# One score product for both heads of a feature tile, and value products on alternating column halves

## Chip, cores and metric

The kernel runs on one core of one Trainium2 chip. The metric is the time of one execution on the device, in microseconds (us); three runs of the kernel before give a median of 3754.48 us (3749.0 to 3759.8). The core has five engines with a queue each: TensorE (PE, matrix products, with weight loads shown apart as PEld), VectorE (DVE), ScalarE (ACT), GpSimd (POOL) and SyncE (SP, which here issues DMA transfers).

## What is computed

The reference is two transformer blocks on 256 tokens of width 2048, all in fp32. The parts that matter here are the two attentions. The first block's attention has an indexer of 8 heads that picks at most 64 keys for each query, and 16 heads of 64 features over keys and values that are expanded from a shared latent:

```python
score = einsum('bqhs,bqh->bqs', relu(einsum('bqhd,bsd->bqhs', qi, ik)), wi)
...
logits = einsum('bqhr,bqkr->bqhk', ql, c_sel) * SA_SCALE + bias
pr = softmax(where(valid, logits, -inf))
o_lat = einsum('bqhk,bqkr->bqhr', pr, c_sel)
```

The second block's attention has 32 query heads of 64 features, four key and value heads (8 query heads share one), a window of 128 keys and a sink per head. Around them stand large projections, a recurrent part (RWKV) and a mixture of experts in the first block, and a state space layer (Mamba) in the second.

## The kernel before, in words

Features lie on the 128 partitions, tokens along the free dimension. A feature tile of 128 partitions holds two heads of 64 features: head 2p in partitions 0 to 63 and head 2p+1 in partitions 64 to 127.

The projections run in `gemm` (line 170): weights come by DMA in `wload`, `wsplit` splits them into a high part on ACT (line 139) and a low part on DVE (line 141), and PE multiplies with the activations (lines 204 and 206, PSUM tile `g`); `gemm_rows` does the same with tokens as rows (lines 227 to 229). Attention works in fp32 without a split, and the profile shows each such product as two passes over the moving columns.

An attention **unit** is one pair of heads and one half of the queries (`tt` 0 or 1, 128 queries each). With `tt` = 0 it has 128 keys, with `tt` = 1 it has 256. A unit of `Dsa.run` (first block) goes like this:

- line 812 loads the bias of both heads (tile `bm`) by a DMA that ACT issues, and line 814 adds the mask on POOL;
- line 819 makes the scores into PSUM tile `psL`, one product for each head, with the 64 partitions of that head as contraction;
- lines 821 to 829 (DVE and ACT) add, take the maximum, exponentiate and normalise;
- line 834 transposes the probabilities on PE into `psP`, and line 836 copies them out on ACT (`pT`);
- line 842 makes the values' products into `psO`, with 64 output partitions for each head;
- lines 846 and 847 write the result as a high and a low part to `o2b` on ACT and DVE.

The pair of a unit are two heads of the same parity, from two neighbouring feature tiles (line 809), so both products of a unit use the same 64 partitions: of the keys as contraction at line 819, and of `psO` as output at line 842. Each head has its own columns in PSUM. `Swa.attend` (second block) does the same for 32 heads: scores at line 1825 (`psl`), softmax at 1831 to 1840, transposes at 1845 (`psp`), values at 1852 (`pso`), and one DVE copy at 1854 into `o`. The indexer of the first block multiplies at line 773 (`psI`) in the same way. There are 16 units in the first block, 32 in the second, and 8 pairs of indexer products.

Keys are prepared once: `ikd` (lines 755 to 757) and `kT` (788 to 796, from `psK`, written by ACT) in the first block, `kd` (1731, filled by DMA at line 1798) in the second. Values `vr` follow `kT` (797 to 805, from `psV`).

`weave` keeps up to three units going and takes one stage of each in turn. All of attention's products share two PSUM banks (tag `m`). The order in each engine's queue is laid out when the kernel is compiled: a scheduler puts instructions that are ready earlier in front of those that are traced before them, so products of the next projections stand between those of the units. Each engine takes its queue in order.

Line 1528 is part of the Mamba layer and isn't touched by the diff; its products have 64 output columns, and consecutive ones (`e` in 0, 1) write different halves of the PSUM partitions:

```python
for ch in range(2):
    for e in range(2):
        E.matmul(ps[64 * e:64 * e + 64, ch * 128:(ch + 1) * 128], lhsT=xd[:, ch, hA + e, :],
                 rhs=M[ch][:, 2 * u + e, :], start=True, stop=True)
```

Of the kernel before, what the change touches and what calls it, by code (L numbers as in the profile page):

```python
# [9 lines left out]
F32 = mybir.dt.float32  # L10
# [4 lines left out]
AF = mybir.ActivationFunctionType  # L15
ALU = mybir.AluOpType
# [4 lines left out]
T = 256  # L21
# [11 lines left out]
DECAY_C = math.exp(-0.5)  # L33
QUAD = "(a b i)"
# [657 lines left out]
SA_SCALE = 64 ** -0.5  # L692
# [18 lines left out]
class Dsa:  # L711
# [23 lines left out]
    def run(self):  # L735
        k, nc, pool, par, c = self.k, self.k.nc, self.pool, self.par, self.k.c
        V, S, P, E = nc.vector, nc.scalar, nc.gpsimd, nc.tensor
# [17 lines left out]
        ikd = pool.tile([128, T], F32, name="ikd")  # L755
        V.tensor_copy(ikd[64:128], kwT[64:128])
        nc.scalar.dma_start(ikd[0:64], kwT[64:128])
# [6 lines left out]
        for tt in range(2):  # L764
            nk = 128 * (tt + 1)
            sc = pool.tile([128, T], F32, name=f"sc{tt}")
            P.memset(sc, 0.0)
            for hq in range(4):
                ps = k.bank("psI")
                for j in range(2):  # L770
                    h = 4 * (hq // 2) + 2 * j + hq % 2
                    hs = slice(64 * (h % 2), 64 * (h % 2) + 64)
                    E.matmul(ps[:, j * 256:j * 256 + nk], lhsT=iqT[h // 2][hs, tt * 128:(tt + 1) * 128],
                             rhs=ikd[hs, 0:nk], start=True, stop=True)
                for j in range(2):
                    h = 4 * (hq // 2) + 2 * j + hq % 2
                    rl = W("rl", [128, T])[:, :nk]
                    V.tensor_scalar(rl, ps[:, j * 256:j * 256 + nk], 0.0, iw[:, tt, h:h + 1], op0=ALU.max, op1=ALU.mult)
# [28 lines left out]
        def unit(tt, hq):  # L807
            nk = 128 * (tt + 1)
            hs_ = [4 * (hq // 2) + 2 * j + hq % 2 for j in range(2)]
            bm = W("bm", [128, 2, T], 3)[:, :, :nk]  # L810
            src = self.bd
            nc.scalar.dma_start(bm, bass.AP(tensor=src.tensor, offset=src.offset + hs_[0] * 512 + 128,
                                            ap=[[1, 128], [1024, 2], [1, nk]]))
            P.tensor_tensor(bm, bm, neg[tt][:, None, :].to_broadcast([128, 2, nk]), op=ALU.add)
            ps = k.bank("psL")
            pv = ps.rearrange("p (j s) -> p j s", j=2)[:, :, :nk]
            for j, h in enumerate(hs_):
                hs = slice(64 * (h % 2), 64 * (h % 2) + 64)
                E.matmul(pv[:, j], lhsT=qT[h // 2][hs, tt * 128:(tt + 1) * 128], rhs=kT[hs, h // 2, T - nk:],
                         start=True, stop=True)  # L820
# [23 lines left out]
            j0, pv = hs_[0] // 2, ps[hs, 0:256].rearrange("p (j t) -> p j t", j=2)  # L844
            hi = self.o2[hs, j0:j0 + 2, tt * 128:(tt + 1) * 128]
            S.copy(hi, pv)
            V.tensor_tensor(self.o2[hs, j0:j0 + 2, T + tt * 128:T + (tt + 1) * 128], pv, hi.bitcast(F32), op=ALU.subtract)

        weave((unit(tt, hq) for tt in range(2) for hq in range(8)), 3, 1)


# [872 lines left out]
class Swa:  # L1724
    def __init__(self, k, par, pool, q):
        self.k, self.par, self.pool, self.q = k, par, pool, q
        nc, a = k.nc, k.a
        self.c = k.load_consts(pool, "const_swa", _SWA)
        self.rot = pool.tile([128, 128], F32R, name="rotr")
        self.o = pool.tile([128, 16, T], F32, name="o")  # L1730
        self.kd = pool.tile([128, 4, T], F32, name="kd")
        self.vr = pool.tile([128, 2, 256], F32, name="vr")
        sk = a["b_sinks_2"]
        self.sk = pool.tile([128, 32], F32, name="sk")
        nc.scalar.dma_start(self.sk, bass.AP(tensor=sk.tensor, offset=sk.offset, ap=[[0, 128], [1, 32]]))

    def tables(self):
# [7 lines left out]
        ang = pool.tile([128, T], F32, name="ang")  # L1745
# [3 lines left out]
        n = pool.tile([128, T], F32, name="nper")  # L1749
# [37 lines left out]
    def evict_kv(self, col, ps):  # L1787
# [25 lines left out]
    def attend(self):  # L1813
# [3 lines left out]
        def unit(hq, tt):  # L1817
            hs_ = [4 * (hq // 2) + 2 * j + hq % 2 for j in range(2)]
            hs = slice(64 * (hq % 2), 64 * (hq % 2) + 64)
            kv = hs_[0] // 8  # L1820
            nk = 128 * (tt + 1)
            ps = k.bank("psl")
            pv = ps.rearrange("p (j s) -> p j s", j=2)[:, :, :nk]
            for j, h in enumerate(hs_):
                E.matmul(pv[:, j], lhsT=self.q[hs, h // 2, tt * 128:(tt + 1) * 128], rhs=self.kd[hs, kv, 0:nk],  # L1825
                         start=True, stop=True)
# [4 lines left out]
            P.tensor_copy(bt[:, :, nk], self.sk[:, hs_[0]:hs_[0] + 3:2])  # L1831
# [17 lines left out]
            ps = k.bank("pso")  # L1849
            for j, h in enumerate(hs_):  # L1850
                for s in range(tt + 1):
                    E.matmul(ps[hs, j * 128:(j + 1) * 128], lhsT=self.vr[:, s, kv * 64:kv * 64 + 64], rhs=pT[:, j, s],  # L1852
                             start=(s == 0), stop=(s == tt))
            V.tensor_copy(self.o[hs, hs_[0] // 2:hs_[0] // 2 + 2, tt * 128:(tt + 1) * 128],
                          ps[hs, 0:256].rearrange("p (j t) -> p j t", j=2))

        weave((unit(hq, tt) for hq in range(16) for tt in range(2)), 3, 1)
# [209 lines left out]
```

## Time and profile before

| | |
|---|---|
| median of three runs | 3754.48 us (3749.0 to 3759.8) |
| the profiled execution | 3757.85 us |
| its span, first to last instruction | 3756.1 us |
| instructions | 56311 |
| PE busy | 3634.1 us, 97% of the span |
| weight loads busy | 3023.4 us, 80% |
| DVE, ACT, POOL busy | 2671.5, 1985.7, 1320.7 us |
| granted TensorE clock, mean | 0.992 |

A row of the time order gives the start, the time from the first start to the last end, the engine, the line, the operation, the tiles written and read, the form and the count. The form `64*128 64x256` is a product with 64 contraction partitions and 128 output partitions over 256 moving columns; `128*64` has 64 output partitions. A row with "x4" merges four such instructions that follow each other. Matmuls are pipelined, so that starts of neighbours lie closer than one's length.

### The profile page before, as it was taken

Reading aid. Unit: us, or ns where it says so; the run is one execution under the profiler, and the core shown is the slowest. Engines: PE = TensorE matmul, PEld = TensorE weight load, DVE = VectorE, ACT = ScalarE, POOL = GpSimd, SP = SyncE. Lnnn points to the kernel's source line nnn. Section 1 sums busy time; section 2 is a strip of 40 time slices with the busy share of each in tenths; the row PEclk is TensorE's granted clock in tenths of the full one; section 3 lists DMA queues with packets and bytes.
Section 4 is the critical chain, followed back from the end, with each engine's and each line's share of the span. In section 5 each row is a group of like instructions: output and inputs, shape, how many; then the busy total and the mean of one; then the engine's idle time right before and its main releaser. Section 6 shows DMA issues by size and latency. Waiting matters only on the chain.

```text
span 3756.1 us, 56311 instructions
## 1 busy us (share of the span) xinstructions
PE 3634.1 (97%) x19927; PEld 3023.4 (80%) x19927; DVE 2671.5 (71%) x4261; ACT 1985.7 (53%) x3739; POOL 1320.7 (35%) x1322
## 2 busy tenths in 40 slices
PE   9999999999999999998899999999999999989998
PEld 7778878878888888877788888887888887878777
DVE  5776767666688888888644444446899879577776
ACT  5445555545454677766444444445555666444553
POOL 1333223321288777655511111112144443151101
PEclk9999999999999999999999999999999999999999
DMA  7453433568598888878777766665544445545334
GB/s 219 125 165 113 130 107 110 169 225 254 166 204 207 199 212 222 210 180 207 232 236 239 239 231 231 223 197 182 180 151 146 153 134 165 184 150 185 124 113 136
DMA packets 358335, 681.24 MB, mean 181 GB/s; under 512 B 43981, under 2 KB 111477, under 8 KB 354853
## 3 DMA queue, kind: packets, MB, share of 16 engines
q1 hardware_dynamic: 305216, 591.50, 53.9%
q10 hardware_dynamic: 52837, 86.14, 6.9%
q8 instruction: 158, 2.59, 0.3%
q14 instruction: 124, 1.02, 0.1%
HBM read 627.57 MB, written 47.22 MB: 180 GB/s over the span
## 4 chain that ended last, share of the span: by engine, by line
PE 45%; DVE 8%; DMA 2%; issue 2%; ACT 2%; POOL 0%; ACTq 0%; DVEq 0%; SPq 0%; POOLq 0%
PE g L204 12%; PE g L206 6%; PE gv L1238 5%; PE gv L1237 5%; PE gv L1236 5%; DVE tr L1176 2%; PE dv L1236 2%; PE dv L1237 2%; PE dv L1238 2%; DVE lo L141 2%; DVE oh L1152 1%; ACT hi L139 1%; PE psl L1825 1%; PE g L228 1%; PE pso L1852 1%
## 5 line engine op out<-in xcount | busy, mean ns | idle before, releaser
L141 DVE TENSOR_TENSOR lo<-raw,hi 128x1024 fp32r<-128x1024 f32 (+3 forms) x856 | 1047.1, 1226 | 697.7 <-ACT hi L139 677.8
L139 ACT CAST hi<-raw 128x1024 fp32r<-128x1024 f32 (+3 forms) x858 | 867.5, 1014 | 979.7 <-PE g L204 345.4
L204 PE MATMUL g<-x,hi 128*128 128x512 f32 x3040 | 1089.3, 400 | 13.2 <-DVE x L1646 9.0
L206 PE MATMUL g<-x,lo 128*128 128x256 f32 x3040 | 842.8, 288 | 11.4 <-DVE lo L141 11.2
L1195 PE MATMUL gu<-x,hi 128*128 128x512 f32 x2048 | 733.7, 398 | 4.1 <-ACT hi L139 4.1
L141 POOL TENSOR_TENSOR lo<-tr,hi 128x512 fp32r<-128x512 f32 x429 | 591.5, 1408 | 262.0 <-ACT hi L139 182.3
L204 PEld LDWEIGHTS g<-x,hi 128*128 128x128 f32 x3040 | 568.2, 189 | 135.6 <-issue 19.6
L206 PEld LDWEIGHTS g<-x,lo 128*128 128x128 f32 x3040 | 574.6, 189 | 46.2 <-DVE lo L141 19.5
L1196 PE MATMUL gu<-x,lo 128*128 128x256 f32 x2048 | 581.6, 284 | 13.2 <-POOL lo L141 9.7
L1195 PEld LDWEIGHTS gu<-x,hi 128*128 128x128 f32 x2048 | 386.9, 189 | 91.1 <-ACT hi L139 5.4
L1196 PEld LDWEIGHTS gu<-x,lo 128*128 128x128 f32 x2048 | 387.7, 189 | 22.2 <-POOL lo L141 16.9
L1176 DVE STREAM_TRANSPOSE tr<-raw 128x1024 f32<-128x1024 f32 x256 | 309.1, 1231 | 88.9 <-POOL lo L141 47.8
L139 ACT CAST hi<-tr 128x512 fp32r<-128x512 f32 x512 | 289.4, 615 | 65.0 <-PE gu L1195 37.0
L141 POOL TENSOR_TENSOR g<-scr,g 128x512 fp32r<-128x512 f32 x64 | 112.2, 1754 | 574.4 <-ACT g L139 574.4
L1238 PE MATMUL gv<-hi,g 128*128 128x512 f32 x756 | 299.7, 396 | 0.0
L1237 PE MATMUL gv<-lo,g 128*128 128x512 f32 x756 | 299.7, 396 | 0.0
L1236 PE MATMUL gv<-hi,g 128*128 128x512 f32 x756 | 238.4, 396 | 0.0
L1204 ACT ACTIVATE act<-act 128x256 f32<-128x256 f32 x128 | 53.4, 417 | 242.2 <-DVE act L240 224.7
L204 PE MATMUL g<-y2m,hi 128*128 128x512 f32 x512 | 173.6, 395 | 0.0
L1238 PEld LDWEIGHTS gv<-hi,g 128*128 128x128 f32 x756 | 142.4, 188 | 34.7
L1237 PEld LDWEIGHTS gv<-lo,g 128*128 128x128 f32 x756 | 142.4, 188 | 34.7
L1236 PEld LDWEIGHTS gv<-hi,g 128*128 128x128 f32 x756 | 142.4, 188 | 34.7
(595 smaller groups left out, 5912.1 us busy)
## 6 DMA issues: line engine op xcount, KB each, us to landing
raw<-in_peer_u_dram SPq DMA_DIRECT2D x512, 256.0 KB
raw<-in_peer_v_dram SPq DMA_DIRECT2D x256, 512.0 KB
raw<-in_a_w_in_dram SPq DMA_DIRECT2D x160, 512.0 KB
raw<-in_w_in_dram SPq DMA_DIRECT2D x136, 512.0 KB
raw<-in_b_w_in_dram SPq DMA_DIRECT2D x64, 512.0 KB
raw<-in_a_w_out_dram SPq DMA_DIRECT2D x48, 512.0 KB
raw<-in_w_out_dram SPq DMA_DIRECT2D x32, 512.0 KB
raw<-in_w_peer_query_dram SPq DMA_DIRECT2D x32, 512.0 KB
```

The source lines that it names most:

```text
L139: ins = nc.scalar.copy(hi, x) if heng == "act" else nc.vector.tensor_copy(hi, x)
L141: return ins, eng.tensor_tensor(lo, x, hi.bitcast(F32), op=ALU.subtract)
L204: nc.tensor.matmul(ps[f], lhsT=hi[:, k, f * 128:(f + 1) * 128], rhs=x2[:, q, :], start=(q == 0), stop=False)
L206: nc.tensor.matmul(ps[f][:, 0:T], lhsT=lo[:, k, f * 128:(f + 1) * 128], rhs=x2[:, q, 0:T], start=False, stop=(q == nk - 1))
L228: nc.tensor.matmul(ps[tt], lhsT=x, rhs=lo[:, k, 0:n], start=False, stop=False)
L1176: st["t"] = nc.vector.transpose(tr.rearrange("p b (u j) -> p u b j", u=2), raw[:, 2 * u:2 * u + 2].rearrange("p u (b j) -> p u b j", j=32))
L1195: nc.tensor.matmul(ps, lhsT=hi[:, j], rhs=self.hn2[:, q, :], start=(q == 0), stop=False)
L1196: st["m"] = nc.tensor.matmul(ps[:, 0:T], lhsT=lo[:, j], rhs=self.hn2[:, q, 0:T], start=False, stop=(q == KT - 1))
L1204: nc.scalar.activation(o, o, AF.Gelu)
L1236: nc.tensor.matmul(p, lhsT=x, rhs=hi, start=first, stop=False)
L1237: nc.tensor.matmul(p, lhsT=x, rhs=lo, start=False, stop=False)
L1238: nc.tensor.matmul(p, lhsT=g2[:, T + tt * 128:T + tt * 128 + 128], rhs=hi, start=False, stop=last)
```

## The change

Heads are paired by feature tile: unit `p` takes heads 2p and 2p+1. Keys are stored twice as wide, `[128, ..., 2, T]`: copy 0 holds head 2p's features in partitions 0 to 63 and zeros below, copy 1 holds head 2p+1's in partitions 64 to 127 and zeros above. So one product with 128 contraction partitions gives both heads' scores side by side. POOL writes the zeros. In the first block ACT writes `kT` in two halves for each PSUM tile. The values' products keep their form with 64 output columns, but consecutive ones now go to different halves of the output partitions, and both heads share the same 128 columns of PSUM, so the result is read as one 128x128 tile. The second block's tables `ang` and `n` take buffers of the later gate tiles.

```diff
-        ikd = pool.tile([128, T], F32, name="ikd")
-        V.tensor_copy(ikd[64:128], kwT[64:128])
-        nc.scalar.dma_start(ikd[0:64], kwT[64:128])
+        ikd = pool.tile([128, 2, T], F32, name="ikd")
+        P.memset(ikd[0:64, 1], 0.0)
+        P.memset(ikd[64:128, 0], 0.0)
+        V.tensor_copy(ikd[64:128, 1], kwT[64:128])
+        nc.scalar.dma_start(ikd[0:64, 0], kwT[64:128])
...
-            for hq in range(4):
-                ps = k.bank("psI")
+            for p in range(4):
+                ps = k.bank("psI")[:, 0:2 * nk].rearrange("p (j s) -> p j s", j=2)
+                E.matmul(ps, lhsT=iqT[p][:, tt * 128:(tt + 1) * 128], rhs=ikd[:, :, 0:nk], start=True, stop=True)
...
-        kT = pool.tile([128, 8, T], F32, name="kT")
+        kT = pool.tile([128, 8, 2, T], F32, name="kT")
+        P.memset(kT[0:64, :, 1], 0.0)
+        P.memset(kT[64:128, :, 0], 0.0)
...
-            S.activation(kT[:, j:j + 2], ps.rearrange("p (u t) -> p u t", u=2), AF.Copy, scale=SA_SCALE)
+            for e, hs in enumerate(HALVES):
+                S.activation(kT[hs, j:j + 2, e], ps.rearrange("p (u t) -> p u t", u=2)[hs], AF.Copy, scale=SA_SCALE)
...
-            ps = k.bank("psL")
-            pv = ps.rearrange("p (j s) -> p j s", j=2)[:, :, :nk]
-            for j, h in enumerate(hs_):
-                hs = slice(64 * (h % 2), 64 * (h % 2) + 64)
-                E.matmul(pv[:, j], lhsT=qT[h // 2][hs, tt * 128:(tt + 1) * 128], rhs=kT[hs, h // 2, T - nk:],
-                         start=True, stop=True)
+            pv = k.bank("psL")[:, 0:2 * nk].rearrange("p (j s) -> p j s", j=2)
+            E.matmul(pv, lhsT=qT[p][:, tt * 128:(tt + 1) * 128], rhs=kT[:, p, :, T - nk:], start=True, stop=True)
...
-            ps = k.bank("psO")
-            hs = slice(64 * (hq % 2), 64 * (hq % 2) + 64)
-            for j, h in enumerate(hs_):
-                for s in range(tt + 1):
-                    E.matmul(ps[hs, j * 128:(j + 1) * 128], lhsT=vr[:, 1 - tt + s, h * 64:h * 64 + 64], rhs=pT[:, j, s],
-                             start=(s == 0), stop=(s == tt))
...
+            ps = k.bank("psO")[:, 0:128]
+            for st in range(tt + 1):
+                for j, hs in enumerate(HALVES):
+                    E.matmul(ps[hs], lhsT=vr[:, 1 - tt + st, p * 128 + j * 64:p * 128 + j * 64 + 64], rhs=pT[:, j, st],
+                             start=(st == 0), stop=(st == tt))
+            hi = self.o2[:, p, tt * 128:(tt + 1) * 128]
+            S.copy(hi, ps)
+            V.tensor_tensor(self.o2[:, p, T + tt * 128:T + (tt + 1) * 128], ps, hi.bitcast(F32), op=ALU.subtract)
...
-        self.kd = pool.tile([128, 4, T], F32, name="kd")
+        self.kd = pool.tile([128, 4, 2, T], F32, name="kd")
+        nc.gpsimd.memset(self.kd[0:64, :, 1], 0.0)
+        nc.gpsimd.memset(self.kd[64:128, :, 0], 0.0)
...
-        ang = pool.tile([128, T], F32, name="ang")
+        ang = pool.tile([128, T], F32, tag="gat", bufs=4, name="ang")
...
-        n = pool.tile([128, T], F32, name="nper")
+        n = pool.tile([128, T], F32, tag="gth", bufs=2, name="nper")
...
-                    nc.scalar.dma_start(self.kd[64 * dst:64 * dst + 64, 2 * j + e], r[64 * e:64 * e + 64])
+                    nc.scalar.dma_start(self.kd[64 * dst:64 * dst + 64, 2 * j + e, dst], r[64 * e:64 * e + 64])
```

The second block's units (lines 1817 to 1857) change in the same way as the first's: one score product against `kd[:, kv, :, 0:nk]`, values with `st` outside and `j` inside, and one DVE copy of `[128, 128]` in place of `[64, 256]`.

## Rows read from the trace of the kernel before

**Rows 1.** Page, part 1: busy time, share of the span, instructions.

```profile
PE 3634.1 (97%) x19927; PEld 3023.4 (80%) x19927; DVE 2671.5 (71%) x4261; ACT 1985.7 (53%) x3739; POOL 1320.7 (35%) x1322
```

**Rows 2.** Stretch, length; busy us of PE, PEld, DVE, ACT, POOL; clock, DMA.

```profile
104.00:135.00 31.00, 30.00 (x127) 20.69 (x127) 26.71 (x85) 9.72 (x16) 14.90 (x25) 1.00 0.18 54
135.00:240.00 105.00, 101.53 (x554) 77.91 (x554) 78.27 (x143) 56.03 (x133) 34.15 (x56) 1.00 0.50 157
3479.00:3682.00 203.00, 201.82 (x1069) 152.82 (x1070) 144.38 (x303) 104.69 (x252) 17.22 (x31) 1.00 0.36 114
```

**Rows 3.** Waits of PE, 100 to 240: us in total, times, longest us.

```profile
PE psP L834 <- DVE bm L829: 3.2, 6, 0.8
PEld psP L834 <- issue: 2.5, 4, 1.1
```

**Rows 4.** Waits of PE's weight loads, 3479 to 3682.

```profile
PEld psp L1845 <- ACT b L1837: 1.1, 1, 1.1
```

**Rows 5.** PE in order of time: start us, first start to last end.

```profile
3492.14 0.28 PE L206 MATMUL g<-x,lo 128*128 128x256 f32 x1
3492.26 0.39 PE L204 MATMUL g<-x,hi 128*128 128x512 f32 x1
3492.49 0.60 PE L1845 MATMUL psp<-const_f,b 128*128 128x128 f32 x4
3493.02 0.71 PE L1825 MATMUL psl<-kd,hh 64*128 64x128 f32 x4
3493.66 0.39 PE L206 MATMUL g<-x,lo 128*128 128x256 f32 x1
3493.88 0.39 PE L204 MATMUL g<-x,hi 128*128 128x512 f32 x1
3494.20 1.09 PE L1852 MATMUL pso<-pT,vr 128*64 128x128 f32 x8
```

**Rows 6.** PE in order of time: first and last stretch of L1825, of L819.

```profile
3480.92 0.71 PE L1825 MATMUL psl<-kd,hh 64*128 64x128 f32 x4
...
3670.99 1.13 PE L1825 MATMUL psl<-kd,hh 64*128 64x256 f32 x4
...
132.91 0.71 PE L819 MATMUL psL<-kT,d 64*128 64x128 f32 x4
...
227.57 1.13 PE L819 MATMUL psL<-kT,d 64*128 64x256 f32 x4
```

**Rows 7.** Matmuls of three lines: count, ns min/median/max, first and last start.

```profile
L773 PE MATMUL psI<-ikd,d x32: 272/375/480, 107.3 to 118.0; 64*128 64x128 f32 x16, 64*128 64x256 f32 x16
...
L842 PE MATMUL psO<-pT,vr x96: 272/273/324, 140.7 to 234.3; 128*64 128x128 f32 x96
...
L1852 PE MATMUL pso<-pT,vr x192: 272/273/324, 3488.4 to 3680.3; 128*64 128x128 f32 x192
```

**Rows 8.** PE in order of time, 119 to 133: fp32 on the whole array.

```profile
119.04 7.07 PE L793 MATMUL psK<-csq,wuk 128*128 128x256 f32 x32
125.95 7.03 PE L802 MATMUL psV<-wuv,csq 128*128 128x512 f32 x16
```

**Rows 9.** PE in order of time: L1528 alternates column halves, L1852 does not.

```profile
2760.62 0.66 PE L1528 MATMUL psy<-m,xd 128*64 128x128 f32 x8
2762.71 0.44 PE L1528 MATMUL psy<-m,xd 128*64 128x128 f32 x4
...
3488.42 0.65 PE L1852 MATMUL pso<-pT,vr 128*64 128x128 f32 x4
```

**Rows 10.** POOL in order of time, idle before in brackets; then line 796.

```profile
47.14 0.56 POOL L767 MEMSET sc<- 128x256 f32 x2
62.52 2.12 POOL L243 TENSOR_TENSOR d<-half,rs_in 128x256 f32<-128x256 f32 x3 [14.82 <-DVE half L242]
...
3386.58 1.44 POOL L1784 TENSOR_TENSOR rpt<-rpt,cos 128x256 f32<-128x256 f32 x2 [10.28 <-PE g L204]
...
L796 ACT ACTIVATE kT<-psK x4: 597/597/597, 121.0 to 126.1; 128x512 f32<-128x512 f32 x4
```

More of the change, by code (lines that the diff above doesn't have):

```diff
@@ L33 @@
 DECAY_C = math.exp(-0.5)
+HALVES = [slice(0, 64), slice(64, 128)]
 QUAD = "(a b i)"
@@ L767, in run @@
             P.memset(sc, 0.0)
-            for hq in range(4):
-                ps = k.bank("psI")
+            for p in range(4):
+                ps = k.bank("psI")[:, 0:2 * nk].rearrange("p (j s) -> p j s", j=2)
+                E.matmul(ps, lhsT=iqT[p][:, tt * 128:(tt + 1) * 128], rhs=ikd[:, :, 0:nk], start=True, stop=True)
                 for j in range(2):
-                    h = 4 * (hq // 2) + 2 * j + hq % 2
-                    hs = slice(64 * (h % 2), 64 * (h % 2) + 64)
[L773 to L776, printed above, removed]
+                    h = 2 * p + j
                     rl = W("rl", [128, T])[:, :nk]
-                    V.tensor_scalar(rl, ps[:, j * 256:j * 256 + nk], 0.0, iw[:, tt, h:h + 1], op0=ALU.max, op1=ALU.mult)
+                    V.tensor_scalar(rl, ps[:, j], 0.0, iw[:, tt, h:h + 1], op0=ALU.max, op1=ALU.mult)
                     P.tensor_tensor(sc[:, :nk], sc[:, :nk], rl, op=ALU.add)
@@ L805, in run, with unit @@
                 S.copy(vr[:, st, u * 512:(u + 1) * 512], ps)
-        def unit(tt, hq):
+        def unit(tt, p):
             nk = 128 * (tt + 1)
-            hs_ = [4 * (hq // 2) + 2 * j + hq % 2 for j in range(2)]
             bm = W("bm", [128, 2, T], 3)[:, :, :nk]
             src = self.bd
-            nc.scalar.dma_start(bm, bass.AP(tensor=src.tensor, offset=src.offset + hs_[0] * 512 + 128,
-                                            ap=[[1, 128], [1024, 2], [1, nk]]))
+            nc.scalar.dma_start(bm, bass.AP(tensor=src.tensor, offset=src.offset + 2 * p * 512 + 128,
+                                            ap=[[1, 128], [512, 2], [1, nk]]))
             P.tensor_tensor(bm, bm, neg[tt][:, None, :].to_broadcast([128, 2, nk]), op=ALU.add)
-            ps = k.bank("psL")
-            pv = ps.rearrange("p (j s) -> p j s", j=2)[:, :, :nk]
-            for j, h in enumerate(hs_):
-                hs = slice(64 * (h % 2), 64 * (h % 2) + 64)
-                E.matmul(pv[:, j], lhsT=qT[h // 2][hs, tt * 128:(tt + 1) * 128], rhs=kT[hs, h // 2, T - nk:],
-                         start=True, stop=True)
+            pv = k.bank("psL")[:, 0:2 * nk].rearrange("p (j s) -> p j s", j=2)
+            E.matmul(pv, lhsT=qT[p][:, tt * 128:(tt + 1) * 128], rhs=kT[:, p, :, T - nk:], start=True, stop=True)
             V.tensor_tensor(bm, pv, bm, op=ALU.add)
@@ L837, in unit @@
             yield
-            ps = k.bank("psO")
-            hs = slice(64 * (hq % 2), 64 * (hq % 2) + 64)
-            for j, h in enumerate(hs_):
-                for s in range(tt + 1):
-                    E.matmul(ps[hs, j * 128:(j + 1) * 128], lhsT=vr[:, 1 - tt + s, h * 64:h * 64 + 64], rhs=pT[:, j, s],
-                             start=(s == 0), stop=(s == tt))
[L844 to L849, printed above, removed]
+            ps = k.bank("psO")[:, 0:128]
[6 more added lines that the diff above has]
+            V.tensor_tensor(self.o2[:, p, T + tt * 128:T + (tt + 1) * 128], ps, hi.bitcast(F32), op=ALU.subtract)
+        weave((unit(tt, p) for tt in range(2) for p in range(8)), 3, 1)
 def branch_b(k, o2, yb_d, pool):
@@ L1816, in attend, with unit @@
         W = lambda n, shape, bufs=3, dt=F32: pool.tile(shape, dt, tag="w_" + n, bufs=bufs, name=n)
[L1817 to L1820, printed above, removed]
+        def unit(p, tt):
+            kv = p // 4
             nk = 128 * (tt + 1)
[L1822 to L1826, printed above, removed]
+            pv = k.bank("psl")[:, 0:2 * nk].rearrange("p (j s) -> p j s", j=2)
+            E.matmul(pv, lhsT=self.q[:, p, tt * 128:(tt + 1) * 128], rhs=self.kd[:, kv, :, 0:nk], start=True, stop=True)
             bt = W("b", [128, 2, T + 1])
@@ L1848, in unit @@
             yield
[L1849 to L1857, printed above, removed]
+            ps = k.bank("pso")[:, 0:128]
+            for st in range(tt + 1):
+                for j, hs in enumerate(HALVES):
+                    E.matmul(ps[hs], lhsT=self.vr[:, st, kv * 64:kv * 64 + 64], rhs=pT[:, j, st], start=(st == 0),
+                             stop=(st == tt))
+            V.tensor_copy(self.o[:, p, tt * 128:(tt + 1) * 128], ps)
+        weave((unit(p, tt) for p in range(16) for tt in range(2)), 3, 1)
     def evict_gate(self, o2, after):
```

2 lines of the change are left out of this document (1 added, 1 removed).

## The prediction

> **What bounds the kernel now.** I read the page's busy time first: TensorE (PE) is busy for 97% of the span, VectorE (DVE) for 71% [rows 1]. A busy PE is not yet a PE at its peak, so I went to the two stretches in which the changed lines run. The first block's attention lies between 104 and 240 us, the second block's between 3479 and 3682; PE is busy for 131.5 of 136 us and for 201.8 of 203 [rows 2]. In both, matrix products of the neighbouring projections (`g`, lines 204, 206, 227 to 229) stand between the attention units and fill PE. Its waits for the softmax are small: 5.7 us at the transposes of the first block [rows 3], the largest of the second block 1.1 us [rows 4]. So both stretches last as long as PE's instructions, and time taken from these instructions shortens the stretch, as long as filling work is there and DVE keeps up.
>
> Then I read PE in order of time, starts against starts, since a row's length includes the end of the pipeline. Where nothing changes, line 206 gives way to line 204 after 0.12 us and line 204 to the next after 0.23 [rows 5]. Four passes of 128 columns take 0.60 us, of which 0.27 is the last one's own length (the median length of line 1852 [rows 7]), so passes start 0.109 us apart. Now the scores: from the first transpose to the first score pass are 0.53 us, not 4 x 0.109 = 0.436, so 0.094 are lost where the array goes from 128 to 64 rows. From the first score pass to line 206 are 0.64: 0.436 for the passes, 0.094 for the way back, and 0.105 for a first weight load that nothing covers. After that line 206 takes 0.22 instead of 0.12, the same open load again [rows 5]. **A visit to the half array between whole-array products costs 4 x about 0.1 = 0.40 us**, 0.20 on the way in and 0.20 on the way out.
>
> **The change part by part. Scores.** Both heads go into one K=128 product against keys with zeros in the other half. Columns streamed stay the same: before 4 passes of 128 or 256 columns (0.44 or 0.86 us), after 2 passes of 256 or 512. The whole-array fp32 rows give 0.216 us per 256 columns ((7.07 - 0.38) / 31, the 0.38 being a 256-column pass's own length, the median of line 773 [rows 7]) and 0.43 per 512 ((7.03 - 0.59) / 15, the 0.59 being 0.38 and 0.216 for 256 more columns) [rows 8]: 0.43 and 0.86. The zeros cost nothing and save nothing. What goes is the visit to the half array. In the order of time line 1825 stands in 39 stretches and line 819 in 22 [rows 6]; line 773 makes 6 visits [rows 7]. Six of the 39 and five of the 22 are followed at once by the values' products, which still switch, so their way out stays. Removed are 39 + 33 switches in the second block and 28 + 23 in the first: 72 x 0.20 = 14.4 us and 51 x 0.20 = 10.2 us.
>
> By a rule of the Trainium skill this would look worse: "TensorEngine Tiling (Array Packing)", section Performance Considerations, wants a contraction of 64 run as two row tiles for up to twice the speed, which padding with zeros gives up. If the old scores overlapped like this, the change would stream twice as long. There is no overlap now, four passes take 0.436 us [rows 5], since both heads of an old unit lie in the same 64 rows, so the sum has no term for it.
>
> **Values.** 192 and 96 passes [rows 7] are 32 and 16 units: half of them (queries 0 to 127) with 4 passes, half with 8. Before, both heads write the same 64 columns: 0.65 - 0.27 = 0.38 us from first to last start for 4 passes [rows 9], 1.09 - 0.27 = 0.82 for 8 [rows 5]. What alternation does is not seen on these lines, but line 1528 has the same form, 128 rows by 64 columns with 128 moving columns, and changes column halves from one product to the next: 0.44 - 0.27 = 0.17 and 0.66 - 0.27 = 0.39 [rows 9]. Bounds for a pair of units are 0 (no overlap) and 0.21 + 0.43 = 0.64 us. I take the upper end, as the row nearest in form and size. Line 1528 differs in that it doesn't accumulate; but accumulating passes are no slower than others now, 0.117 us apart with the first open load in it (0.82 / 7) [rows 5]. 16 pairs give 10.2 us, 8 pairs 5.1.
>
> **Evictions and pads.** One 128x128 read takes the place of 64x256 after each unit, on ACT and DVE, half the columns; that work lies beside PE, so I count nothing. The first block's keys now leave PSUM in 8 ACT copies for 4 at 0.60 us [rows 10], at most 2.4 us more; ACT is busy for 9.7 of 31 us there [rows 2] and the next products (lines 793 and 802, 14.1 us without a break [rows 8]) need only a free bank: the 8 passes of a bank take 1.7 us and cover its two copies, 1.2. With that cover gone the first scores come 1.2 us later. POOL clears `ikd`, `kT` and, in the second block, `kd`. A 128x256 clear takes at most 0.31 us (two in 0.56) [rows 10], so 8 x 0.31 x 2 = 5.0 us for `kT`, 0.6 for `ikd`, 2.5 for `kd`, from above; from below, nothing. `kT` and `ikd` can go where the score clears went, at 47 us, in front of 14.8 idle us of POOL; behind them waits the scaling of line 243. `kd` comes before the rotation of line 1784, which has 10.3 idle us ahead of it [rows 10]. The scores' product now waits for clear and copy of both halves, all long done by then. Without this cover 5.6 us would be lost in the first block and 2.5 in the second; with it, zero. The bias loads, the key copies by DMA, `ang` and `n` in shared buffers keep their number and their queues: zero.
>
> **Sum.** PE gives back 14.4 + 10.2 = 24.6 us in the second block and 10.2 + 5.1 = 15.3 in the first, 39.9 together. Not all of it lands. DVE's work stays, so its share grows from 144.4 of 203 us to 144.4 of 178, 81%, and from 105 of 136 to 105 of 121, 87% [rows 2]. PE will wait more for split weights and softmax. As an estimate I double today's first-block waits, 5.7 us more [rows 3], and add one longest wait, 1.1 us [rows 4], for the second: 39.9 - 6.8 = 33 us. The profiled execution took 3757.85 us for its 3756.1 us span, 3.4 above the median of 3754.48; it would become 3725, and the median 3721.5. I say 3722.
>
> **Rivals. DVE takes over in the first block.** For it: 87% leaves little room and a unit's chain of maximum, exponent and normalisation goes through DVE four times. Against it: PE's waits there are 5.7 us now at a DVE share of 77% (105 of 136), and the share rises by ten points, not to 100. Then only the second block's 23.5 us land: 3731. The Trainium skill names this way too ("TensorEngine Tiling (Array Packing)", section PSUM Bottleneck): faster products leave the reading of PSUM as the limit. DVE has some 13% left there by the shares above [rows 2], so it's a rival and not the forecast.
>
> **The halves do not overlap**, because two accumulations share a bank: the change doesn't do what it says for the values. 15.3 us less: 39.9 - 15.3 - 6.8 = 18 us gained, 3737. Line 1528 speaks against it.
>
> **No net gain.** The order of instructions is laid out anew at compile time, and PE takes its queue in order. Where a unit's transposes stand too early, PE waits for that softmax with filling work queued behind it. The longest such waits now are 1.1 us [rows 3, 4]. If each of the 48 units waited 0.83 us more, the 39.9 us would be used up: about 3754.
>
> **Slower.** The same place, further on: each unit waits 1.1 us more at its transposes and then 0.2 more at the values' products, for the ACT copy: 48 x 1.3 = 62 us, 22 more than is saved: 3777. It decides from 0.83 + 11.3 / 48 = 1.07 us per unit on. Against it: today's waits occur ten times in the first block [rows 3] and once at that length in the second [rows 4], and a shorter PE share per unit leaves the same filling work between them.
>
> **How the numbers follow.** A measurement of this kernel tells a change from none from about 0.3%, 11.3 us; faster then means under 3743.2. Chances: forecast 0.66, DVE 0.12, no overlap 0.05, no net gain 0.10, slower 0.07. The first three are faster, 0.83, and the fourth the same, 0.10. The range begins where all 39.9 us land, 3714.6, less the 5.5 us by which the lowest run lies under the median, 3709; it ends at 3742, past DVE and the halves, so that the last two cases, 0.17, are left out.
>
> **What would show it.** In the profile after, scores of the form 128\*128 with 256 or 512 columns, two passes each; no open load before or after them; value stretches of 0.44 and 0.66 us in place of 0.65 and 1.09; the stretch from the first score of the second block to its last values' product shorter by 20 to 25 us. Value stretches still at 0.65 and 1.09 would prove the halves wrong; transposes with waits near 1 us at most units would prove the order wrong; POOL clears after 104 us or late in the second block would prove the pads wrong. The prediction is wrong if the order of the filling work changes so far that one stretch no longer ends with PE full.

## The result, and the profile after

The changed kernel takes 3734.22 us (median of five runs, 3731.29 to 3736.59), the kernel before 3754.81 beside it (3749.0 to 3759.8): a ratio of 0.9935 with a 95% interval of 0.9924 to 0.9946. That is 20.6 us less by the medians, 23.6 between the two profiled executions, 24 by the ratio. The forecast was 32.8 less. The experiments below ran beside runs of the kernel before of 3760 to 3762 us, so they are compared by their ratios.

The page of the kernel after, its head and the line of busy times, against [rows 1]:

```profile
span 3732.4 us, 56118 instructions
PE 3596.9 (96%) x19815; PEld 2991.2 (80%) x19815; DVE 2663.3 (71%) x4261; ACT 1990.3 (53%) x3745; POOL 1329.2 (36%) x1328
```

PE's busy time falls by 37.2 us, more than the span's 23.7. The stretches of the kernel after, against [rows 2]; the last one is the rest behind the second attention. The columns are stretch, length, then busy us (and count) of PE, PEld, DVE, ACT and POOL, then clock, DMA share and GB/s:

```profile
104.00:135.00 31.00, 28.80 (x112) 19.16 (x113) 26.68 (x85) 12.58 (x21) 14.84 (x25) 1.00 0.18 54
135.00:237.00 102.00, 92.98 (x532) 69.49 (x531) 74.67 (x142) 54.30 (x134) 37.81 (x53) 0.98 0.52 166
3476.00:3653.00 177.00, 175.20 (x985) 130.47 (x983) 134.06 (x300) 102.18 (x250) 11.75 (x31) 1.00 0.39 125
3653.00:3732.00 79.00, 66.42 (x382) 56.55 (x378) 49.23 (x76) 27.36 (x46) 17.30 (x12) 0.92 0.45 147
```

The first block's stretch now shows a PE with 9 us idle of 102, where [rows 2] had 3.5 of 105. The second block's went from 203 to 177 us and looks as full as before. That fullness misleads: a busy time built from overlapping lengths hides short waits, and the order of time shows them. PE of the kernel after, second block, against [rows 5, 9]:

```profile
3562.49 0.28 PE L207 MATMUL g<-x,lo 128*128 128x256 f32 x1
3562.84 0.68 PE L1839 MATMUL psp<-const_f,b 128*128 128x128 f32 x4
3563.36 0.60 PE L1820 MATMUL psl<-kd,hh 128*128 128x256 f32 x2
3563.60 0.58 PE L205 MATMUL g<-x,hi 128*128 128x512 f32 x1
3564.02 0.28 PE L207 MATMUL g<-x,lo 128*128 128x256 f32 x1
...
3564.37 0.28 PE L207 MATMUL g<-x,lo 128*128 128x256 f32 x1
3564.58 0.66 PE L1846 MATMUL pso<-pT,vr 128*64 128x128 f32 x8
...
3570.42 0.44 PE L1846 MATMUL pso<-pT,vr 128*64 128x128 f32 x4
```

The scores are one product of two passes on the whole array. Their first pass starts 0.11 us behind the last transpose (median of the second block; 0.20 before), as one transpose behind another: nothing is lost on the way in. The start of line 205, 0.24 us later, doesn't measure the way out, since the two passes alone need 0.43. The product behind it, line 207, does: it starts 0.67 us after the first score pass, 0.43 for the scores and 0.23 for line 205, so nothing is lost there either. The values stretch over 0.66 and 0.44 us, just as line 1528 did in [rows 9]; less the last pass's 0.27 that is 0.39 and 0.17 from first to last start, against 0.82 and 0.38 before. Counted in the order of time, PE changes the part of the array that it works on 481 times before and 358 times after (a change from one part to another counts too): 123 fewer, and 72 + 51 = 123 were forecast.

The matmuls and the pads of the kernel after, by tile (count, ns minimum, median and maximum, first and last start), against [rows 6, 7, 10]:

```profile
L1820 PE MATMUL psl<-kd,hh x64: 379/520/595, 3476.6 to 3645.6; 128*128 128x256 f32 x32, 128*128 128x512 f32 x32
L839 PE MATMUL psO<-pT,vr x96: 272/273/476, 139.5 to 231.7; 128*64 128x128 f32 x96
L1846 PE MATMUL pso<-pT,vr x192: 272/273/324, 3483.7 to 3652.9; 128*64 128x128 f32 x192
L798 ACT ACTIVATE kT<-psK x8: 592/592/595, 120.6 to 126.4; 64x512 f32<-64x512 f32 x8
L788 POOL MEMSET kT<- x1: 1806/1806/1806, 48.3 to 48.3; 64x2048 f32 x1
L1728 POOL MEMSET kd<- x1: 948/948/948, 3347.9 to 3347.9; 64x1024 f32 x1
```

From the first score to the last values' product the second block takes 3652.9 - 3476.6 = 176.3 us, after 3680.3 - 3480.9 = 199.4 [rows 6, 7]: 23 us less, as forecast (20 to 25). The rest behind it gives 3.7 us back (3756.1 - 3680.3 = 75.8 before, 3732.4 - 3652.9 = 79.5 after). Behind the start of the last values' product stand six more products (378 for 372), as many as the shorter attention holds fewer as filling (628 for 634), and the mean clock is 0.92 for 0.94. The stretches of the rows hold 382 and 370, since they begin at different distances from that product. The rest behind the attention in the kernel before, in the same columns:

```profile
3681.00:3756.00 75.00, 62.98 (x370) 53.49 (x368) 47.53 (x77) 26.44 (x46) 13.87 (x12) 0.94 0.45 146
```

In the first block the last values' product starts at 231.7 instead of 234.3 us [rows 7]: only 2.6 us earlier, where 9.6 were forecast. But this stretch holds more filling now, and the next product outside attention (`psA`) stands at 244.1 for 249.2, 5.1 us earlier.

What landed in each attention shows when the filling is made equal, at the 0.23 us from start to start of a product with 512 columns and the 0.12 of one with 256 [rows 5]. In the second block 23.1 us less with six products of 512 columns fewer are 21.7 us. In the first, from the first indexer product to the last values' product, 129.7 - 127.1 = 2.6 us less with 14 products more (372 for 358, seven pairs of 0.35 us) are 5.1. Together that is 26.7 us. Taking the 39.9 as right, 13 didn't land, 3 of them in the second block and 10 in the first, where the sum had 6.8.

The waits show where. Three fences follow, each with what waits, for whom ("issue": for nothing that the profile shows), us in total, times and the longest. First the weight loads of the kernel before, in 104 to 240 and 3480 to 3681, beyond those of [rows 3, 4]:

```profile
PEld psO L842 <- ACT pT L836: 2.2, 7, 0.3
...
PEld psO L842 <- issue: 2.0, 8, 0.3
...
PEld pso L1852 <- issue: 6.9, 24, 0.4
...
PEld pso L1852 <- ACT pT L1847: 1.7, 5, 0.4
```

The weight loads of the kernel after, in 104 to 237 and 3476 to 3653:

```profile
PEld psP L832 <- DVE bm L827: 10.8, 11, 3.3
PEld psO L839 <- ACT pT L834: 8.3, 15, 1.5
...
PEld psO L839 <- issue: 1.3, 1, 1.3
...
PEld pso L1846 <- ACT pT L1841: 12.2, 25, 0.9
...
PEld pso L1846 <- issue: 1.2, 5, 0.3
```

And its products and its POOL, in 104 to 237:

```profile
PE psP L832 <- DVE bm L827: 7.6, 9, 3.0
...
POOL bm L816 <- DMA bm<-bias_d: 27.5, 8, 5.7
```

The values now wait for ACT's copy of the transposed probabilities in 40 of 48 units, 20.5 us in all, where it was 3.9 in 12 units. Not all of this is new: at the same loads the time that waits for nothing fell from 8.9 us (6.9 + 2.0) to 2.5. The first block's transposes wait for the softmax's last step on DVE, 10.8 us at the loads; the 7.6 us at the products, where it was 3.2 [rows 3], are part of the same waits and don't add to them. A load's wait is not all idle PE, since an earlier product can still run. Counted in the order of time, as what starts lie apart beyond the spacing of the same product without a wait, PE's waits grow from 7.6 to 20.9 us in the first block and from 4.6 to 11.8 in the second, by 20.5 us (the same figure as the copies' waits, by chance). That count hangs on the spacing that is taken as free of waits, with others it gives 19 to 24, and it is more than the 13 us that are missing in time.

One of these waits also cost clock. PE of the kernel after in order of time, idle before and its releaser in brackets:

```profile
214.54 0.39 PE L205 MATMUL g<-x,hi 128*128 128x512 f32 x1
217.95 1.12 PE L832 MATMUL psP<-const_f,bm 128*128 128x128 f32 x4 [3.02 <-DVE bm L827]
```

The stretch of that wait and the one behind it, in the columns of the stretches above:

```profile
214.50:218.00 3.50, 0.48 (x4) 0.17 (x2) 1.65 (x3) 0.87 (x1) 3.27 (x6) 0.96 0.20 72
218.00:221.40 3.40, 3.40 (x14) 1.81 (x14) 2.21 (x4) 0.59 (x1) 2.26 (x2) 0.54 0.33 71
```

After 3.02 us without a product the granted clock is 0.54 for the next 3.4 us, the lower of its two levels (1.2 GHz) for nearly all of it.

### The profile page after: what moved, and what is told of

Read it like the earlier page. It is cut to its first block, busy times and chain, and to the rows that moved or that the text cites. A ratio compares the mean times of both kernels' runs of the same rounds, so it can differ in the third digit from the quotient of the medians.

```text
span 3732.4 us, 56118 instructions
## 1 busy us (share of the span) xinstructions
PE 3596.9 (96%) x19815; PEld 2991.2 (80%) x19815; DVE 2663.3 (71%) x4261; ACT 1990.3 (53%) x3745; POOL 1329.2 (36%) x1328
## 4 chain that ended last, share of the span: by engine, by line
PE 45%; DVE 8%; issue 2%; ACT 1%; DMA 1%; POOL 0%; ACTq 0%; DVEq 0%; POOLq 0%
PE g L205 12%; PE g L207 6%; PE gv L1234 5%; PE gv L1233 5%; PE gv L1232 5%; DVE tr L1172 2%; DVE lo L142 2%; PE dv L1233 2%; PE dv L1232 2%; PE dv L1234 2%; DVE oh L1148 1%; ACT hi L140 1%; PE g L229 1%; PE g L230 1%; PE g L228 1%
## 5 line engine op out<-in xcount | busy, mean ns | idle before, releaser
L207 PE MATMUL g<-x,lo 128*128 128x256 f32 x3040 | 843.5, 288 | 12.0 <-DVE lo L142 11.4
L207 PEld LDWEIGHTS g<-x,lo 128*128 128x128 f32 x3040 | 574.0, 189 | 47.7 <-DVE lo L142 21.7
```

The costliest lines, as they stand in the source:

```text
L207: nc.tensor.matmul(ps[f][:, 0:T], lhsT=lo[:, k, f * 128:(f + 1) * 128], rhs=x2[:, q, 0:T], start=False, stop=(q == nk - 1))
```

## The experiments

**Each block alone.** `second_only` keeps the first block and its indexer as before, `first_only` the second block; the rest is the changed kernel.

```diff
second_only
-        kT = pool.tile([128, 8, 2, T], F32, name="kT")
+        kT = pool.tile([128, 8, T], F32, name="kT")
...
first_only
-        self.kd = pool.tile([128, 4, 2, T], F32, name="kd")
+        self.kd = pool.tile([128, 4, T], F32, name="kd")
...
```

> The change in the second block alone, the first block as before. From the two traces, the second block's stretch gave 19 us of the whole, and only about 4 us were left of the first block's part after the mixture of experts. Theory A (the second block holds nearly all): 3735 to 3738 us. Theory B (the loss of 5 us in the mixture of experts was chance, and both blocks count): about 3744.

> The change in the first block alone. Theory A: 3750 to 3753 us, and in the trace the last values' product of the first block ends within 3 us of where it ended before (234 us), since that attention is not bound by TensorE. Theory B: about 3745.

Measured: `second_only` 3740.52 us, ratio 0.9944 (0.9931 to 0.9957), some 21 us less than before. `first_only` 3754.4 us, 0.9981 (0.9973 to 0.999), some 7 us less. The larger part is the second block's, near its forecast of 23.5; the first gives about 7 of 9.6. Together that is 28, and the whole change gave 24; the intervals allow both. At the first chip's level of 3754.8 us the ratios make 3734 and 3748: a little under theory A for `second_only`, between A and B for `first_only`, so neither theory comes out whole. The waits go with the block. Weight loads of `second_only`, 3484 to 3661:

```profile
PEld pso L1851 <- ACT pT L1846: 12.6, 27, 0.8
```

Weight loads of `first_only`, 104 to 237:

```profile
PEld psP L832 <- DVE bm L827: 11.4, 10, 3.3
PEld psO L839 <- ACT pT L834: 7.2, 15, 0.8
```

**The scores alone.** Whole-array scores against the padded keys, but a product for each head, pairs of one parity, and the values' products as before.

```diff
-            E.matmul(pv, lhsT=qT[p][:, tt * 128:(tt + 1) * 128], rhs=kT[:, p, :, T - nk:], start=True, stop=True)
+            for j, h in enumerate(hs_):
+                E.matmul(pv[:, j], lhsT=qT[h // 2][:, tt * 128:(tt + 1) * 128], rhs=kT[:, h // 2, h % 2, T - nk:],
+                         start=True, stop=True)
```

> Scores on the whole array in both blocks, but one product for each head with the old pairs, and the values as before: only the visits to the half array go, 24.6 of the 39.9 us of TensorE's instructions. If the visits cost what the rows of before show and land in the same share as the whole change (0.52): 3742 us, with no open weight load around the scores. If the gain came from the overlap of the values' products instead: 3750 or more.

Measured: 3746.79 us, 0.9961 (0.9949 to 0.9973), some 15 us less (10 to 19 by the interval), with 358 changes of the array's part, as many as the full change; at the first chip's level that is 3740 us, where 3742 was expected. So the scores give 15 us of the forecast 24.6, and the values, by the difference to 0.9935, some 10 of 15.3 (4 to 16). The values are as slow as before here, and yet they wait for the copies as soon as the visits are gone, 7.2 us in 24 units of the second block (1.7 in 5 before), and start 0.24 us after the copy's end (median), where it was 0.55 before and is 0.23 in the changed kernel. Weight loads of `scores_only`, 3482 to 3671:

```profile
PEld pso L1858 <- ACT pT L1853: 7.2, 24, 0.4
```

**A stage between copy and values.** If the values wait for their own copy, a unit more in flight should take it away.

```diff
             S.copy(pT[:, :, 0:tt + 1], ps.rearrange("p (j s t) -> p j s t", j=2, s=2)[:, :, 0:tt + 1])
             yield
+            yield
...
-        weave((unit(p, tt) for p in range(16) for tt in range(2)), 3, 1)
+        weave((unit(p, tt) for p in range(16) for tt in range(2)), 4, 1)
```

(The first block likewise, and `pT` in three buffers.)

> The changed kernel with one more round between the copy of the transposed probabilities and the values' products, four units going instead of three. Theory C (what did not land is waits that the visits to the half array had covered: the copy by ACT before the values' products, 8.3 us in the first block and 12.2 in the second): these waits fall under 3 us in each block and the time to 3722 to 3728 us. Theory D (VectorE's load sets the pace, so any order waits): the waits move to the transposes, and the time stays at 3732 to 3736.

Measured: 3738.26 us, 0.9942 (0.9929 to 0.9954), not to be told from the changed kernel: the time that theory D gives, but the waits stay at the values, and D wants them at the transposes. Weight loads of `lag`, 3482 to 3659:

```profile
PEld pso L1848 <- ACT pT L1842: 10.4, 30, 0.8
```

Yet each unit's own copy had ended some 5.5 us before its values (median). In 30 of the 32 units they start 0.05 to 0.4 us after the copy of the next unit's transposes. The theory as it stood falls: what the values wait for there is not their operand but the PSUM bank, of the two that attention has, which that copy empties.

**Another bank for the values.** Three kernels take the values' PSUM tile from the projections' banks (tag `g`): alone, with the added stage, and with six buffers for the bias as well.

```diff
-            ps = k.bank("pso")[:, 0:128]
+            ps = k.gp.tile([128, 512], F32, tag="g", name="pso")[:, 0:128]
```

> The changed kernel with the values' products in a PSUM bank of the projections' six instead of the attention's two. The values still follow their own unit's transposes at once, so the copy of these probabilities stays ahead of them. Theory E (two things hold the values back, their own copy and the bank that it empties, and either alone is enough): waits before the values' products stay at 8 and 12 us, time 3732 to 3738 by the first chip's level. Theory F (the bank alone): waits under 3 us and 8 to 12 us less time.

> The same bank for the values and one more round between copy and values, so neither the copy nor its bank is just ahead. Theory E: waits before the values' products fall from 8.3 and 12.2 us to under 2 in each block, and the time falls by 8 to 14 us against the changed kernel, to 0.990 or 0.991 of the kernel before. Theory D (VectorE's load sets the pace): the waits turn up before the transposes and the ratio stays near 0.994.

> As before it, with six bias tiles instead of three in the first block, so that bias loads and mask additions can run ahead. If the first block's softmax waits before the transposes (10.8 and 7.6 us in the changed kernel) come from POOL's wait for the bias (27.5 us), they fall by more than half and the values of the first block end 8 us earlier or more. If they come from VectorE's chain, nothing moves by more than 2 us.

Measured: 3896.39 us, 1.036 (1.0345 to 1.0374); 3900.19, 1.0366 (1.0352 to 1.0381); 3900.88, 1.0372 (1.0358 to 1.0386). All miss what was expected, and they decide nothing about the bank, since they changed something larger. The projections' products now wait their turn in the same rotation of banks as the values, and in the second block none stands between two units any more. `own_bank`, second attention and the stretch behind it:

```profile
3526.00:3694.00 168.00, 99.14 (x357) 50.75 (x356) 66.34 (x196) 47.32 (x162) 6.75 (x31) 0.50 0.00 0
3694.00:3790.00 96.00, 95.85 (x543) 82.86 (x544) 56.07 (x86) 48.92 (x86) 0.00 (x0) 0.98 0.50 165
```

Waits of PE and of its loads in the former of the two:

```profile
PE psp L1839 <- DVE b L1834: 50.6, 32, 4.3
PEld pso L1846 <- ACT pT L1841: 40.4, 31, 1.5
```

The last three columns of a stretch are clock, DMA share and GB/s. The 32 units alone take 168 us with the clock at 0.50 throughout, nearly as long as units and filling together in the changed kernel (177). What had been filling comes behind them, 543 products in the next 96 us. A third bank for attention wasn't tried, so what the bank itself is worth stays open.

**One half after the other.** The values' products of head 0 all come before those of head 1.

```diff
-            for st in range(tt + 1):
-                for j, hs in enumerate(HALVES):
+            for j, hs in enumerate(HALVES):
+                for st in range(tt + 1):
```

> The changed kernel with the loops of the values' products swapped: all key blocks of one head, then of the other. With 128 keys the order is the same as in the changed kernel; with 256 keys each half gets two products in a row. If the overlap needs neighbours on different halves, the 8-pass stretches rise from 0.39 us to between 0.6 and 0.82 from first to last start, 24 units x 0.2 to 0.43 = 5 to 10 us of TensorE's time, of which half or less shows in the whole: ratio up by 0.001. If the halves run free of the order, they stay at 0.39.

Measured: 3737.27 us, 0.993 (0.9916 to 0.9944), as the changed kernel. PE in order of time of `halves_in_turn`:

```profile
3502.45 0.66 PE L1846 MATMUL pso<-pT,vr 128*64 128x128 f32 x8
3507.13 0.44 PE L1846 MATMUL pso<-pT,vr 128*64 128x128 f32 x4
```

Still 0.66 us for eight passes, although four of one half now stand ahead of four of the other. Single starts in the trace bear out that the order did change: the second half's first pass starts 13 to 14 ns behind the first half's, with four passes ahead of it, and 6 to 7 ns in the changed kernel, with two. That neighbours have to alternate falls: what counts is that a unit's heads use different halves. The Trainium skill agrees in part ("TensorEngine Tiling (Array Packing)", Key Properties: different tiles can load and multiply in parallel).

**Faster copies.** ACT copies head 0's transposes, DVE head 1's.

```diff
-            S.copy(pT[:, :, 0:tt + 1], ps.rearrange("p (j s t) -> p j s t", j=2, s=2)[:, :, 0:tt + 1])
+            pv = ps.rearrange("p (j s t) -> p j s t", j=2, s=2)
+            S.copy(pT[:, 0, 0:tt + 1], pv[:, 0, 0:tt + 1])
+            V.tensor_copy(pT[:, 1, 0:tt + 1], pv[:, 1, 0:tt + 1])
```

> The changed kernel with the copy of the transposed probabilities shared: head 0 by ACT, head 1 by DVE, so that it takes about 0.37 us instead of 0.58 with 256 keys and 0.26 instead of 0.37 with 128. Theory G (the values' products wait for this copy, now that the visits to the half array no longer cover it): from the last transpose to the first values' product 0.1 to 0.2 us less, waits before the values' products down from 8 and 12 us to about 5 and 8, time down by 3 to 7 us, ratio 0.9915 to 0.993. Theory D (VectorE's load sets the pace): DVE gets 48 more instructions, some 14 us, and the ratio rises to 0.995 or more.

Measured: 3739.93 us, 0.9938 (0.9925 to 0.9952), no gain. The waits did shrink: the values of the second block wait 4.8 us for DVE where they waited 12.2 for ACT, and start 0.78 us (median) after ACT's copy, now of one head, instead of 0.23. Weight loads of `copy_split`, 3483 to 3666:

```profile
PEld pso L1850 <- issue: 4.2, 15, 0.4
PEld pso L1850 <- DVE pT L1845: 3.0, 9, 0.8
...
PEld pso L1850 <- DVE b L1828: 1.8, 6, 0.4
```

A values' stretch of eight passes of `copy_split` that is broken in two, in the order of time:

```profile
3497.36 0.43 PE L1850 MATMUL pso<-pT,vr 128*64 128x128 f32 x2
3497.72 0.49 PE L205 MATMUL g<-x,hi 128*128 128x512 f32 x1
3498.15 0.65 PE L1850 MATMUL pso<-pT,vr 128*64 128x128 f32 x6
```

What was saved came back in another form. The heads' halves become ready apart, so the compiler's order puts filling work between them in 11 of the 48 units (38 values' stretches for 32 in the second block, 21 for 16 in the first): 380 changes of the array's part for 358. Loads with nothing to wait for ("issue") cost 4.2 us at the values where it was 1.2. From the first score to the end the second block takes 3740.6 - 3483.8 = 256.8 us, the changed kernel 3732.4 - 3476.6 = 255.8; the first block, from the first indexer product to the last values' product, 133.1 us for 127.1, with 393 filling products for 372. As far as these traces show, a wait for the copy and a visit more are two prices for the same 0.2 to 0.4 us.

**More bias buffers, and both.** `bias6` gives the first block's bias and score tile six buffers for three; `split_bias6` adds the split copies.

```diff
-            bm = W("bm", [128, 2, T], 3)[:, :, :nk]
+            bm = W("bm", [128, 2, T], 6)[:, :, :nk]
```

> The changed kernel with six bias tiles instead of three in the first block. Theory H (the first block's transposes wait for a softmax that waits for its bias): POOL's wait for the bias (27.5 us) falls under 10, the waits before the transposes from 10.8 to under 5, the first block's values end 5 us earlier or more. Theory I (the chain through DVE and the PSUM banks sets the rate): POOL waits less, and nothing else moves by more than 2 us.

> Both edits. If both theories G and H hold, the gains add: 6 to 12 us under the changed kernel. If G alone: as with the shared copy.

Measured: `bias6` 3733.88 us, 0.9927 (0.9913 to 0.994); `split_bias6` 3731.63 us, 0.9921 (0.9907 to 0.9934). Both intervals overlap the changed kernel's. In `bias6` the bias comes earlier and the transposes wait a little less, 9.4 us at the loads for 10.8 and 6.4 at the products for 7.6. That is short of theory H, which wanted POOL's wait under 10 us and the loads' under 5. POOL, products and loads of `bias6`, 104 to 236:

```profile
POOL bm L816 <- DMA bm<-bias_d: 17.0, 6, 4.8
...
PE psP L832 <- DVE bm L827: 6.4, 9, 1.5
...
PEld psP L832 <- DVE bm L827: 9.4, 11, 1.9
```

From the first indexer product to the last values' product its first block takes 228.9 - 105.0 = 123.9 us, the changed kernel 231.7 - 104.6 = 127.1, and the profiled spans differ by the same 3.1 us. That size fits a bias that came late, but one profile of each is all there is for it: the runs can't tell 3 us. `split_bias6` has the lowest time of all kernels here, faster than the kernel before; whether it beats the changed one stays open.

**A visit put back.** Before the values' products of every unit one small product on 64 rows, whose result the values overwrite.

```diff
             ps = k.bank("pso")[:, 0:128]
+            E.matmul(ps[:, 0:64], lhsT=self.q[0:64, p, tt * 128:(tt + 1) * 128], rhs=self.kd[0:64, kv, 0, 0:64],
+                     start=True, stop=True)
```

> Added to the changed kernel: before the values' products of each of the 48 units one product on 64 rows (64x128 weights, 64 columns), whose result the values overwrite. By the prices of before (0.094 us for one switch more, 0.105 us for an open load, 0.053 us for 64 columns) that is 0.25 us of PE each, 12 us in all. Cover theory (in the changed kernel 40 of the 48 units' values wait for the copy of pT, 20.5 us in all, 0.5 us each, because the visits that stood there are gone): PE goes through the added visit while it would have waited, the waits shrink by about 8 to 10 us, and the time grows by 2 to 4 us (ratio to before 0.993 to 0.995, hardly to be told from the changed kernel's 0.9935). Rival (the waits are no loss, something else holds the gain back): the added PE work counts whole, 12 us, 3746 us, ratio about 0.9965 to 0.997.

Measured: 3740.27 us, 0.9949 (0.9935 to 0.9962), 5 us above the changed kernel with overlapping intervals. Weight loads of `visit_back`, 3476 to 3660:

```profile
PEld pso L1845 <- ACT pT L1842: 11.7, 26, 0.8
```

PE of `visit_back` in order of time:

```profile
3485.09 0.43 PE L1845 MATMUL pso<-kd,hh 64*128 64x64 f32 x2
3485.45 0.66 PE L1848 MATMUL pso<-pT,vr 128*64 128x128 f32 x8
```

The added visit costs 0.36 us, not the 0.25 worked out (two passes), so 48 would add 17 us. It didn't stand inside the wait as meant: it waits for the copy itself, 11.7 us in 26 units, although it reads nothing that the copy writes. That leaves the bank. So the test says little about the cover, but two things about the rest: the bank that a unit's copy empties holds PE even where the operand isn't needed, and of the 17 us of added PE work some 5 show. With both intervals that is -1 to 12: 17 is out, the rival's 12 lies at the edge.

## Why the prediction was right or wrong

**The scores' visits: right in kind and number.** The products have the form that was named, nothing is lost beside them, and 123 changes went, as counted. Two row tiles at once, the other way that the prediction names, weren't run. **The values: right.** 0.17 and 0.39 us for 0.38 and 0.82 are the upper end that was taken from line 1528 [rows 9]. The rival in which the halves don't overlap is out; accumulation in one bank doesn't hinder it.

**Pads and evictions: right.** POOL clears `ikd` and `kT` between 47 and 52 us and has 10.6 idle us after them; `kd` is cleared at 3348, long before its first use. ACT's eight key copies take 0.59 us each and the values' evictions lie beside PE; the second block's DVE copy fell from 0.42 to 0.28 us.

**DVE as the bound: wrong.** Its share is 76% in both blocks' stretches (26.68 + 74.67 of 133 us, 134.06 of 177), not 87 and 81. The rival that names it gives 3731, nearer to the measured 3734 than the forecast, but by chance: it lets none of the first block's saving land, and 5 to 7 us did. The waits point to the latency of a unit's chain, not to DVE's load. That is the way of the two rivals with long waits at each unit, at a smaller size: 13 / 48 = 0.27 us per unit, where no net gain needed 0.83.

**The step that failed is the last term of the sum, the waits that keep part of the saving from landing: 6.8 us forecast, some 13 measured.** At equal filling 10 us are missing in the first block, where the sum had 5.7, and 3 in the second, where it had 1.1. Another 3 lie outside the two attentions: 26.7 us landed in them and 23.6 between the profiled executions. The waits as counted, 20.5 us, don't close the sum. They would leave 15.3 - 13.3 = 2.0 us of gain in the first block, where the trace has 5.1 and `first_only` 7, and 24.6 - 7.2 = 17.4 in the second, where the trace has 21.7 and `second_only` 21. That 39.9 - 20.5 = 19.4 comes near the 20.6 by the medians is luck.

The working doubled the first block's waits and added one wait of 1.1 us for the second. Of the 5.7 us that it doubled, 2.5 are "issue" and no wait for the softmax [rows 3], and the waits at the values were left out. It took the waits of before as a measure of how close the chain was, and that they don't tell. The order of PE is nearly the same in both kernels: transposes, the next unit's scores, up to five filling products, values. ACT's copy ends 0.9 us after the last transpose starts in both. Before, the values started 1.41 us after that transpose (median, second block; 1.30 in the first), because the visit to the half array lay between, and so half a microsecond after the copy. After, they start at 1.10 (1.06), as soon as the copy is done and its bank free. The visits that the change removes were the cover of the copy. The prediction has a wait for this copy only in its rival "Slower", 0.2 us a unit, and names no work that hides it. `scores_only` shows it apart from the values' own change.

This is the larger wait in the second block, and all that is missing there is 3 us. In the first block the transposes also wait for the softmax, whose bias comes late: 10.8 us at the loads, 7.6 of products standing still. Which of the two waits costs the 10 us there isn't shown; with the bias earlier (`bias6`) most of the second one stayed.

**Where the rest stands.** That these waits are the missing gain is read from the traces; no experiment turned them into time. `lag` kept them, since they are for the bank as much as for the operand; `copy_split` removed most of the second block's and paid with visits; `visit_back` met the same bank. Between 1009 and 3340 us nothing of the change runs, and from there to 3476 only the second block's clears, tables and key loads. The expert's first product stands at 1009.1 us after, at 1018.8 before and at 1013.6 in `second_only`, whose first block is that of before; by the second block's first score the lead of the changed kernel is down from 9.7 to 4.3 us. Differences of 5 us there are chance in one execution.

## What to carry to other kernels

Work that a change takes out of an engine's queue may be what covers a neighbour's latency: for each removed piece, look at what lies behind it in the queue and how long that is already ready when its turn comes. Here the values started 25.9 us after their copies before, added up over the 48 units, and 11.4 us after. The waits of the kernel before don't show this slack; the distance between the end of the producer and the start of the consumer does. What the lost slack costs isn't the sum of the new waits, since part of them took the place of waits that stood there before under "issue". Compare the stretch before and after at equal filling instead.

## What the runs showed that was not expected

- Products on different column halves overlap even when four passes of one half stand ahead of four of the other: 0.39 us from first to last start in either order, 0.82 on one half (`halves_in_turn`).
- Without filling work between them the second block's 32 units took 168 us at a granted clock of 0.50, nearly the 177 of units and filling together, and the kernel 3.6% longer than before (`own_bank`).
- A product that needs only a free PSUM bank waits as long as one that needs the copied data (11.7 and 12.2 us, `visit_back` and the changed kernel).
